# RMSNorm with SiLU on one core: the first store cut into four one-row transfers, two constants filled by GpSimd

## The chip, the core and the metric

The kernel runs on one core of a Trainium2 chip. The metric is the device time of one execution in microseconds (us). Before the change the median of three runs is 316.97 us (316.86 to 317.07).

A core has TensorE (matmuls), VectorE (DVE in the profile), ScalarE (ACT), GpSimd (POOL) and SyncE (SP, which here only issues DMAs). Sixteen DMA engines move data between the memory of the chip (HBM) and the core's working memory (SBUF, 128 partitions).

## The reference

The input x is 8 x 1024 x 2048 in float32, gamma has 2048 elements. Each of the 8192 rows is divided by its root mean square, multiplied by gamma, and put through SiLU:

```
rms = np.sqrt(np.mean(x ** 2, axis=-1, keepdims=True) + eps)
out = gamma * x / rms
return (out * (1 / (1 + np.exp(-out)))).astype(np.float32)
```

67.1 MB are read and 67.1 MB written.

## The kernel before, in words

The rows are cut into 16 blocks of 512. In a block each of the 128 partitions holds J = 4 rows that follow one another in HBM, so that a partition's part of a block is one run of 4 x 2048 float32 = 32 KB, and a block is 4 MB. Six buffers (BUFS) of that size lie in SBUF. `load(b)` (L54) is one DMA issued from ACT's queue into the next buffer; `store(b)` (L102) is one DMA issued from SP's queue out of it. The work is done in place in the buffer. Load b+6 goes into the buffer of block b, and so waits until store b has landed.

For each block there are these steps:

- `squares_scalar` (L65) and `squares_vector` (L73): the sums of squares of the four rows, one or two rows on ACT and the rest on VectorE.
- `root` (L82, ACT) and `invert` (L87, VectorE): square root of the mean plus eps, and its reciprocal.
- `multiply` (L92, VectorE): row times reciprocal times gamma, a row at a time.
- `silu` (L98, ACT): two instructions, each over two rows of a partition (128 x 4096); then the store.

The order is written out by hand (`manual_schedule`), and each engine works its own instructions in that order; an instruction that waits holds what is behind it in its engine's queue. ACT's queue holds the issues of the loads too: `squares_scalar(b + 1, loads)` issues load b+3 right behind the first of its rows, for b from 3 on. SP's queue holds gamma's DMA (L110) and then the 16 stores in order, each behind a wait for its block's last SiLU.

Ahead of the loop, load 0 is issued (L106). Then `ones` (128 x 128) and `eps_t` (128 x 1) are filled by VectorE (L107, L108). ACT squares one column of ones (L109), and TensorE multiplies ones by gamma (L113) to spread gamma over all partitions; VectorE copies the result (L115). Load 1 is issued behind L109, and loads 2 to 5 behind an ACT instruction that waits for that copy (L116). The last block is treated in a somewhat different order (L152 to L159) and ends with one store.

Of the kernel before, what the change touches and what calls it, by code (L numbers as in the profile page):

```python
# [1 line left out]

# [4 lines left out]

ACT = mybir.ActivationFunctionType
ALU = mybir.AluOpType


@with_exitstack
def kernel(
    ctx: ExitStack,
    tc: tile.TileContext,
    x: bass.AP,
    gamma: bass.AP,
    eps: bass.AP,
    out: bass.AP,
):  # L20

    nc = tc.nc
    P = nc.NUM_PARTITIONS
    f32 = mybir.dt.float32
    x2 = x.flatten_outer_dims()
    o2 = out.flatten_outer_dims()  # L30
    n, d = x2.shape
    J = 4
    BUFS = 6
    nblk = n // (P * J)
    xb = x2.rearrange("(b p j) d -> b p (j d)", p=P, j=J)
    ob = o2.rearrange("(b p j) d -> b p (j d)", p=P, j=J)

    singles = ctx.enter_context(tc.tile_pool(name="singles", bufs=1))
    pool = ctx.enter_context(tc.tile_pool(name="pool", bufs=BUFS))
    small = ctx.enter_context(tc.tile_pool(name="small", bufs=2))  # L40
    psum = ctx.enter_context(tc.tile_pool(name="psum", bufs=1, space=bass.MemoryType.PSUM))

    Q = 4
    w = d // Q
    g = singles.tile([P, d], f32)
    eps_t = singles.tile([P, 1], f32)
    ones = singles.tile([P, P], f32)
    junk_a = psum.tile([P, d], f32, name="junk_a")
    junk_v = psum.tile([P, d], f32, name="junk_v")
    blocks, sss, rmss, rstds = {}, {}, {}, {}  # L50

    def load(b):
        xt = pool.tile([P, J * d], f32, name="xt")
        nc.scalar.dma_start(out=xt, in_=xb[b])  # L54
        blocks[b] = xt

    def row(b, j):
        return blocks[b][:, j * d:(j + 1) * d]

    def squares_scalar(b, loads=()):  # L60


        sss[b] = small.tile([P, J], f32, name="ss")
        for j in range(share(b)):
            nc.scalar.activation(out=junk_a, in_=row(b, j), func=ACT.Square,  # L65
                                 accum_out=sss[b][:, j:j + 1])
            if j == 0:
                for s in loads:
                    load(s)

    def squares_vector(b):
        for j in range(share(b), J):
            nc.vector.tensor_tensor_reduce(  # L73
                out=junk_v, in0=row(b, j), in1=row(b, j), scale=1.0, scalar=0.0,
                op0=ALU.mult, op1=ALU.add, accum_out=sss[b][:, j:j + 1])

    def share(b):
        return 1 if 4 <= b <= 12 and b % 2 == 0 else 2

    def root(b):  # L80
        rms = small.tile([P, J], f32, name="rms")
        nc.scalar.activation(out=rms, in_=sss.pop(b), func=ACT.Sqrt, scale=1.0 / d, bias=eps_t)  # L82
        rmss[b] = rms

    def invert(b):
        rstd = small.tile([P, J], f32, name="rstd")
        nc.vector.reciprocal(out=rstd, in_=rmss.pop(b))  # L87
        rstds[b] = rstd

    def multiply(b):  # L90
        for j in range(J):
            nc.vector.scalar_tensor_tensor(out=row(b, j), in0=row(b, j), scalar=rstds[b][:, j:j + 1],  # L92
                                           in1=g, op0=ALU.mult, op1=ALU.mult)

    def silu(b):
        for h in range(0, J, 2):
            cols = slice(h * d, (h + 2) * d)
            nc.scalar.activation(out=blocks[b][:, cols], in_=blocks[b][:, cols], func=ACT.Silu)  # L98
        store(b)

    def store(b):
        nc.sync.dma_start(out=ob[b], in_=blocks[b])  # L102

    with tc.manual_schedule():

        load(0)  # L106
        nc.vector.memset(ones, 1.0)  # L107
        nc.vector.memset(eps_t, float(eps))  # L108
        nc.scalar.activation(out=junk_a[:, 0:1], in_=ones[:, 0:1], func=ACT.Square)  # L109
        nc.sync.dma_start(out=g[0:1, :], in_=bass.AP(tensor=gamma.tensor, offset=gamma.offset, ap=[[d, 1], [1, d]]))  # L110
        for c in range(Q):
            cols = slice(c * w, (c + 1) * w)
            nc.tensor.matmul(junk_v[:, cols], ones[0:1, :], g[0:1, cols], start=True, stop=True)  # L113
        load(1)
        nc.vector.tensor_copy(out=g, in_=junk_v)  # L115
        nc.scalar.copy(out=junk_a[:, 0:1], in_=junk_v[:, d - 1:d])  # L116
        for b in range(2, BUFS):
            load(b)

        last = nblk - 1
        SOON = 3
        squares_scalar(0)
        squares_vector(0)
        root(0)
        invert(0)
        for b in range(last):
            loads = [b + 3] if BUFS <= b + 3 < nblk else []
            if b < SOON:  # L130
                multiply(b)
                squares_scalar(b + 1, loads)
                silu(b)
                squares_vector(b + 1)
                root(b + 1)
            elif b < last - 1:
                squares_scalar(b + 1, loads)
                squares_vector(b + 1)
                root(b + 1)
                multiply(b)  # L140
                silu(b)
            else:
                multiply(b)
                squares_scalar(b + 1)
                silu(b)
                squares_vector(b + 1)
                root(b + 1)
            if b + 1 < last:
                invert(b + 1)


        for j in range(J):  # L152
            if j == J // 2:
                invert(last)
            nc.vector.tensor_mul(out=row(last, j), in0=row(last, j), in1=g)  # L155
        for j in range(J):
            nc.scalar.activation(out=row(last, j), in_=row(last, j), func=ACT.Silu,  # L157
                                 scale=rstds[last][:, j:j + 1])
        store(last)  # L159


# [1 line left out]
_INS = ['x', 'gamma', 'eps']  # L163
_OUTS = [((8, 1024, 2048), 'float32')]

_NUMBERS = {'eps': 9.999999747378752e-06}


# [26 lines left out]
```

## Time and profile before

| What | Before |
|---|---|
| Median of three runs | 316.97 us (316.86 to 317.07) |
| Span of the profiled execution, first to last instruction | 315.1 us |
| What lies between the two | 1.9 us |
| HBM read, written | 67.12 MB, 67.11 MB |
| Mean over the span | 426 GB/s |
| First store issued, last store issued | 35.2 us, 300.9 us |
| Load 6 (the first into a used buffer) issued | 66.7 us |

The profile gives a time of its own for the span alone; the runs' time includes what lies ahead of the first instruction and behind the last one.

The page has a row for each engine's busy time, a picture of the span in 40 slices (one digit each, busy tenths; 9 is 90% or more), the DMA queues with packets, MB and the share of the 16 engines' time, and the chain of work that ended last. The view of windows gives, for a stretch, its length, the busy time of each engine (in brackets the number of its instructions), TensorE's granted clock, the busy share of the DMA engines (over 1 where packets that start in the stretch end behind it) and GB/s. A line of the timeline has start, duration, engine (ACTq and SPq are the queues that issue DMAs), line of the code, operation, out<-in, count. The trace also holds every DMA packet with queue, size, start and duration; a packet here is one partition's run.

### The profile page before, as it was taken

What the parts mean: (1) busy time and instruction counts of PE and PEld (TensorE: products, weight loads), DVE (VectorE), ACT (ScalarE), POOL (GpSimd) and SP (SyncE); (2) the same over time, 40 slices, a digit from 0 to 9 for tenths busy, and PEclk for the clock granted to TensorE, in tenths of its full rate; (3) what the DMA queues carried; (4) which work ended last, traced back from release to release, by engine and by line L of the source; (5) the groups of instructions that cost most, each with busy time, mean ns of one, the idle gap of its engine ahead of it and who ended that gap; (6) DMA issues with size and microseconds to landing.
All of it is one profiled execution on the core that took longest, in us unless ns stands there. A gap on an engine that the chain in (4) does not pass through costs nothing.

```text
span 315.1 us, 439 instructions
## 1 busy us (share of the span) xinstructions
PE 7.2 (2%) x8; PEld 2.5 (1%) x8; DVE 235.3 (75%) x157; ACT 213.9 (68%) x137; POOL 0.2 (0%) x4
## 2 busy tenths in 40 slices
PE   6200000000000000000000000000000000000000
PEld 2000000000000000000000000000000000000000
DVE  0679697979895695957969489593995939999600
ACT  1269998972799258682687827877278768779910
POOL 0000000000000000000000000000000000000000
DMA  8999999999999999999999999999999999999997
GB/s 334 412 453 416 383 458 408 462 403 462 403 459 408 454 412 458 408 462 403 462 403 462 408 458 408 458 408 458 416 449 416 449 416 449 428 437 428 437 428 308
DMA packets 4613, 134.24 MB, mean 426 GB/s; under 512 B 514, under 2 KB 514, under 8 KB 514
## 3 DMA queue, kind: packets, MB, share of 16 engines
q10 hardware_dynamic: 2304, 67.11, 49.8%
q1 hardware_dynamic: 2306, 67.12, 49.3%
q14 instruction: 3, 0.02, 0.0%
HBM read 67.12 MB, written 67.11 MB: 426 GB/s over the span
## 4 chain that ended last, share of the span: by engine, by line
DMA 68%; DVE 14%; ACT 11%; issue 1%; ACTq 1%; DVEq 0%
DMA xt<-in_x_dram 68%; DVE xt L92 9%; DVE junk_v L73 5%; ACT xt L98 4%; ACT junk_a L65 3%; ACT xt L157 2%; ACT L82 1%; ACTq L190 1%; ACT L157 0%; ACT L98 0%; ACT rms L82 0%; DVE ss L73 0%; ACTq L54 0%; DVE rstd L87 0%; ACT L109 0%
## 5 line engine op out<-in xcount | busy, mean ns | idle before, releaser
L92 DVE SCALAR_TENSOR_TENSOR xt<-xt,rstd,g 128x2048 f32<-128x2048 f32 x60 | 137.0, 2346 | 0.1
L98 ACT ACTIVATE xt<-xt 128x4096 f32<-128x4096 f32 x30 | 108.3, 3615 | 27.4 <-DVE xt L92 27.4
L73 DVE CUSTOM_DVE_ANT_0 junk_v<-xt 128x2048 f32<-128x2048 f32 x37 | 85.1, 2299 | 42.9 <-DMA xt<-in_x_dram 42.2
L65 ACT ACTIVATE junk_a<-xt 128x2048 f32<-128x2048 f32 x27 | 50.7, 1876 | 16.1 <-DMA xt<-in_x_dram 14.0
L82 ACT ACT_TABLE_LOAD x15 | 19.2, 1283 | 26.6 <-DVE ss L73 26.5
L98 ACT ACT_TABLE_LOAD x14 | 18.0, 1283 | 0.2
L115 DVE COPY g<-junk_v 128x2048 f32<-128x2048 f32 x1 | 2.3, 2292 | 9.0 <-PE junk_v L113 9.0
L87 DVE RECIPROCAL rstd<-rms 128x4 f32<-128x4 f32 x16 | 2.7, 172 | 8.4 <-ACT rms L82 8.4
L155 DVE TENSOR_TENSOR xt<-xt,g 128x2048 f32<-128x2048 f32 x4 | 8.9, 2277 | 0.0
L82 ACT ACTIVATE rms<-ss,eps_t 128x4 f32<-128x4 f32 x16 | 4.8, 297 | 5.7 <-DVE ss L73 5.5
L157 ACT ACTIVATE xt<-xt,rstd 128x2048 f32<-128x2048 f32 x4 | 7.7, 1991 | 0.0
L113 PE MATMUL junk_v<-g,ones 1*128 1x512 f32 x8 | 7.2, 1072 | 2.8 <-DMA g<-in_gamma_dram 2.8
L116 ACT COPY junk_a<-junk_v 128x1 f32<-128x1 f32 x1 | 0.1, 144 | 9.8 <-DVE g L115 9.8
L73 DVE DVE_READ_ACCUMULATOR2_ANT ss<- 128x1 f32 x37 | 5.2, 141 | 0.0
L65 ACT ACTIVATION_READ_ACCUMULATOR junk_a<-xt 128x1 f32 x27 | 5.0, 186 | 0.0
L113 PEld LDWEIGHTS junk_v<-g,ones 1*128 1x128 f32 x8 | 2.5, 325 | 5.9 <-issue 5.9
L109 ACT ACT_TABLE_LOAD x1 | 1.3, 1283 | 1.1 <-PEq L176 1.1
L157 ACT ACT_TABLE_LOAD x1 | 1.3, 1283 | 0.0
L107 DVE MEMSET ones<- 128x128 f32 x1 | 0.2, 165 | 0.8 <-PEq L176 0.8
L109 ACT ACTIVATE junk_a<-ones 128x1 f32<-128x1 f32 x1 | 0.2, 174 | 0.0
L176 POOL MEMSET const-bfloat16-1.0<- 128x1 bf16 x1 | 0.1, 103 | 0.0
L176 POOL MEMSET const-uint8-127<- 128x1 uint8 x1 | 0.1, 102 | 0.0
(3 smaller groups left out, 0.3 us busy)
## 6 DMA issues: line engine op xcount, KB each, us to landing
xt<-in_x_dram ACTq DMA_DIRECT2D x16, 4096.0 KB, 38.7
out_dram<-xt SPq DMA_DIRECT2D x16, 4096.0 KB, 29.0
g<-in_gamma_dram SPq DMA_DIRECT2D x1, 8.0 KB
```

Of the source, the lines that this page charges most:

```text
L65: nc.scalar.activation(out=junk_a, in_=row(b, j), func=ACT.Square, accum_out=sss[b][:, j:j + 1])
L73: nc.vector.tensor_tensor_reduce(out=junk_v, in0=row(b, j), in1=row(b, j), scale=1.0, scalar=0.0, op0=ALU.mult, op1=ALU.add, accum_out=sss ...
L82: nc.scalar.activation(out=rms, in_=sss.pop(b), func=ACT.Sqrt, scale=1.0 / d, bias=eps_t)
L87: nc.vector.reciprocal(out=rstd, in_=rmss.pop(b))
L92: nc.vector.scalar_tensor_tensor(out=row(b, j), in0=row(b, j), scalar=rstds[b][:, j:j + 1], in1=g, op0=ALU.mult, op1=ALU.mult)
L98: nc.scalar.activation(out=blocks[b][:, cols], in_=blocks[b][:, cols], func=ACT.Silu)
L109: nc.scalar.activation(out=junk_a[:, 0:1], in_=ones[:, 0:1], func=ACT.Square)
L113: nc.tensor.matmul(junk_v[:, cols], ones[0:1, :], g[0:1, cols], start=True, stop=True)
L115: nc.vector.tensor_copy(out=g, in_=junk_v)
L155: nc.vector.tensor_mul(out=row(last, j), in0=row(last, j), in1=g)
L157: nc.scalar.activation(out=row(last, j), in_=row(last, j), func=ACT.Silu, scale=rstds[last][:, j:j + 1])
L190: with _tile.TileContext(nc) as tc:
```

## The change

Store 0 is no longer one DMA of 32 KB runs. Behind each half of block 0's SiLU, SP issues two DMAs of one row each (128 partitions x 8 KB). All other stores stay as they were. The two constants are filled by GpSimd instead of VectorE.

```
@@ silu(b)
         for h in range(0, J, 2):
             cols = slice(h * d, (h + 2) * d)
             nc.scalar.activation(out=blocks[b][:, cols], in_=blocks[b][:, cols], func=ACT.Silu)
-        store(b)
+            if b == 0:
+                for j in (h, h + 1):
+                    nc.sync.dma_start(out=ob[b][:, j * d:(j + 1) * d], in_=row(b, j))
+        if b:
+            store(b)
@@ start
         load(0)
-        nc.vector.memset(ones, 1.0)
-        nc.vector.memset(eps_t, float(eps))
+        nc.gpsimd.memset(ones, 1.0)
+        nc.gpsimd.memset(eps_t, float(eps))
```

## The prediction

> **What bounds the kernel now.** I read the page from the top, then the windows, the timeline and the records of single DMA packets. The page first:
>
> ```profile
> span 315.1 us, 439 instructions
> PE 7.2 (2%) x8; PEld 2.5 (1%) x8; DVE 235.3 (75%) x157; ACT 213.9 (68%) x137; POOL 0.2 (0%) x4
> ...
> DMA  8999999999999999999999999999999999999997
> ...
> q10 hardware_dynamic: 2304, 67.11, 49.8%
> q1 hardware_dynamic: 2306, 67.12, 49.3%
> ```
>
> No compute engine is full, but the DMA row holds a 9 in all but the first and last slice, and the two queues (q10 the loads issued by ACT, q1 the stores issued by SP) together occupy the 16 engines for 99.1% of the span. The chain of waits says the same: 68% of it is the loads of xt. Next, the windows by stage; the last two numbers of a row are DMA share and GB/s:
>
> ```profile
> 29.20:35.20 6.00, 0.00 (x0) 0.00 (x0) 4.75 (x5) 5.98 (x3) 0.00 (x0) 1.00 1.01 437
> 35.20:39.50 4.30, 0.00 (x0) 0.00 (x0) 2.67 (x3) 4.26 (x5) 0.00 (x0) 1.00 0.96 328
> ...
> 60.00:280.00 220.00, 0.00 (x0) 0.00 (x0) 176.30 (x118) 150.46 (x93) 0.00 (x0) 1.00 1.00 434
> ```
>
> Loads alone run at 437 GB/s and loads with stores at 434: the engines move the same bytes a second whatever the mix. Only the 4.3 us in which the first store joins are poorer, by 4.3 x (1 - 328/434) = 1.05 us.
>
> The packet records give the same as a sum. A DMA here is 128 packets of 32 KB, 8 on each engine, and a packet follows the last one after 1.210 us. 256 packets are 309.8 us. The first starts 1.8 us into the span and it and its neighbours are stretched by 1.2; the first store costs every engine 0.9 to 1.0; two 8 KB instruction fetches add 0.3 on one engine; from the last packet to the end are 1.2. Sum 315.2, against a span of 315.1. The median of the three runs, 316.97, is 1.9 longer than the span; I take those 1.9 as fixed, and forecast changes on the median.
>
> So only three things can move the time: bytes per second, the 0.9 at the first store, and a stretch in which both queues are empty. Compute counts only through the last.
>
> **The change, part by part.** The places are these rows of the timeline:
>
> ```profile
> 28.03 7.12 ACT L98 ACTIVATE xt<-xt 128x4096 f32<-128x4096 f32 x2
> ...
> 35.18 0.37 SPq L102 DMA_DIRECT2D out_dram<-xt  x1
> ...
> 66.72 0.34 ACTq L54 DMA_DIRECT2D xt<-in_x_dram  x1
> ```
>
> *The constants.* VectorE's memset of ones takes 0.165 us and ends at 0.99, that of eps_t 0.06. GpSimd's four one-column memsets take 0.10 each; none of 128x128 is shown, so the cost is between 0.1 and a value I can't read. It hardly matters: ones is first used by ACT at 2.43 (after a table load) and by TensorE at 2.75 (gamma lands at 2.5), so 1.7 us after 0.8 are covered. Were GpSimd slower, load 1 and loads 2 to 5 would be issued later than 1.21 and 12.38, but their packets' turns come at 12.0 and 21.7; nine more microseconds are covered. Cost 0; VectorE saves 0.2 us where it waits until 10 anyway.
>
> *The issue.* Three more DMA issues on SP, 0.33 us each: two at 31.65 (end of the first half of Silu), two at 35.18. SP's next work, store 1, comes at 49.83. Cost 0. The waits behind them are the Silu halves, which SP awaited before as well.
>
> *Three more completions per engine.* The 4-byte packet that ends a DMA takes 9 ns: 0.03 us.
>
> *Smaller packets.* Store 0 becomes 32 packets of 8 KB per engine instead of 8 of 32 KB. The nearest rows are the 8 KB instruction fetches within the run, recorded with 0.309 us, while a 32 KB packet is recorded with 1.213. A period is 3 ns shorter than its record, so 32 x 0.306 - 8 x 1.210 = 0.11 us. The other end comes from what these fetches took from their engine: the neighbouring packets were stretched so that the fetches cost 0.36 and 0.42 us, 0.05 and 0.12 more than 8 KB at 27.1 bytes/ns (0.303); 32 times that is 1.7 to 3.9 us. I take 0.11, as those two were a third queue's packets, fetched one at a time.
>
> The Trainium skill ("DMA: Bandwidth & Descriptors", section Anatomy of one DMA) speaks against cutting transfers: about 2.0 us fixed per DMA plus bytes at 436 GB/s. By that, were the costs in series, three more DMAs would be an estimated +6 us. This trace disagrees for queued ones: from store 13's last packet to store 14's first (293.38 to 293.75 on the earliest engines) nothing is lost.
>
> *The turn-taking.* With both queues full the records alternate, one load packet, one store packet. With 8 KB on one side a round is 1.210 + 0.306 = 1.516 us, of which the loads get four fifths. The first store packet, 4.4 us after its issue before, comes at about 36.1 instead of 39.6. 27 of the first six loads' 48 packets per engine have then started; the other 21 take 21 x 1.516 and end at 68 (83.7 before). By then 21 of 32 store packets are out, the other 11 go alone until 71.3, and with 1.5 us to land (as before) store 0 is done at 72.8 instead of 58.6. That is later than 66.72, when ACT issues load 6 into the same buffer. So ACT's queue stands 6 us at L54, with root(4) behind it; but root(4) needs VectorE's squares, which end at 75.4. 2.6 us of cover are left. Load 7, issued at 85.3, will wait for store 1 (ends near 86, lands 87.6): 2.3 us late, and beside it VectorE squares rows until 90. From there each load waits for its store; loads and stores both move every 19.4 us, and the next load is queued some 8 us before the last one ends.
>
> What is late next? The load queue is empty from 68 to about 76. The store queue isn't: the rest of store 0, store 1 (issued at 49.8) and store 2 (65.5) lie in it, so the engines stay full. The loads then run ahead: load 15 ends near 270 instead of 277.6, so the last store, issued at 300.9 for a turn at 303.4, gets some 7 us more cover. The end is still bytes over rate.
>
> Sum: 0 + 0 + 0.03 + 0.11 = +0.14, **317.1 us**. The 0.9 of the first store I leave as it is, only 3.5 us earlier.
>
> **The rivals.**
>
> *A. Rejoining costs (slower).* The load queue runs empty and comes back at about 76 among running stores, the mirror of the first store among running loads. If each join stops the engines, load 6 brings 0.55 (mean stretch of load 0's first packets) to 1.0: +0.7 to +1.1, 317.7 to 318.1. For it: both starts in this trace were dear. Against it: both were first uses, and no row shows a rejoin. It decides from the point where load 5 ends before store 0 has landed, 68 against 72.8 here. If the engines took turns otherwise, say so that a row's 8 packets pass together, the queue wouldn't run dry and A falls.
>
> *B. Dear small packets (slower).* 0.05 or more lost per 8 KB: +1.7 to +3.9, 318.7 to 320.9.
>
> *C. A cheaper first store (faster).* If the 0.9 is the filling of a pipe by the store's first packet, a packet of a quarter fills it with less: down to -0.7 with the 0.14 paid, 316.3. Against it: the 32 KB of store 1 may ask for the rest later.
>
> *D. The half store holds ACT.* If the second half of Silu had to wait until rows 0 and 1 have been read out (16 rounds of 1.516 from 36.1 on, landing near 62), ACT would stop for 30 us and both queues would run empty: store 1, 14.7 us after store 0, is then issued near 80 and store 2 near 96, while the 5 us of rows 2 and 3 and the loads are out by 72: 8 + 5 us idle, about 330. Against it: on block 1 Silu's first half starts at 42.00 while VectorE still multiplies rows 2 and 3 (to 46.15), so waits go by rows of a tile, not by the tile.
>
> *E. The fixed cost per DMA,* here three more joints in the store queue. If a joint stopped the engines until the last transfer had landed (1.5 us after its last packet), that were 4.6 with the 0.14, 321.6. Against it: 15 such joints in this trace show no gap, and the loads' packets would fill one. This is the page's rule as a mechanism of this kernel.
>
> **How the numbers follow.** Forecast 0.50 (317.1, within 0.2%); A 0.23; B 0.10; C 0.13; D 0.02; E 0.02. 0.2% is 0.63 us, about what a measurement of this kernel can tell from no change. A lies beyond it (317.60) with 0.18 of its 0.23, B, D and E wholly (0.14); C is beyond 316.34 with about half (0.07). Slower 0.32, faster 0.07, same the rest, 0.61. The range runs from C's end to B's lower end, 316.2 to 318.7; outside are the dear part of B, D and E.
>
> **What would show it.** In the profile after: the DMA row still 9 throughout, q1 with 2,738 packets instead of 2,306 (384 more of data, 48 more of completion); the first store issues at 31.65 and 35.18; load 6 issued at 72 to 73 rather than 66.72 and root(4) not later than 75.6; GB/s near 434 from 40 on, with a poorer window near 76 if A holds and between 36 and 71 if B does; the window of the first store at 32 to 36 as poor as before unless C holds. A SP or ACT wait of tens of microseconds at 32 would be D. The forecast is wrong if any slice in the middle loses its 9, or if 8 KB packets have a period over 0.32 us.

## The result, and the profile after

The changed kernel takes 318.02 us (median of six runs, 317.81 to 319.34); the kernel before, beside it, 317.02 (316.83 to 317.23). The ratio is 1.0042, with a 95% interval of 1.0029 to 1.0055: slower by 1.0 us, clear of the 0.2% that the prediction called no change. The profiled execution took 318.19, of which its span is 316.4; the span is 1.3 longer than before.

The page of the changed kernel, the lines that answer to those shown of before:

```profile
span 316.4 us, 447 instructions
...
DMA  8999999999999999999999999999999999999995
...
q10 hardware_dynamic: 2304, 67.11, 49.5%
q1 hardware_dynamic: 2738, 67.12, 49.2%
```

The DMA row still has its 9s in every slice but the ends, and q1 has the 2,738 packets that were forecast. So the 1.3 us are no gap that a slice would show.

The timeline of the changed kernel around the change (rows of its queues, of GpSimd and of root(4)):

```profile
0.73 0.20 POOL L111 MEMSET ones<- 128x128 f32 x1 [0.29 <-POOLq L180]
...
31.66 4.33 SPq L101 DMA_DIRECT2D out_dram<-xt  x4
...
71.63 0.34 ACTq L54 DMA_DIRECT2D xt<-in_x_dram  x1
...
75.56 0.30 ACT L82 ACTIVATE rms<-ss,eps_t 128x4 f32<-128x4 f32 x1 [5.50 <-DVE ss L73]
```

GpSimd fills ones in 0.20 us and is done long before ACT's first use. The first store is issued at 31.66, load 6 at 71.63 instead of 66.72, and root(4) runs at 75.56, as before: the wait of ACT's queue was covered. The view of waits shows the new order of things:

```profile
ACT junk_a L65 <- DMA out_dram<-xt: 30.3, 4, 7.8
...
ACT L82 <- DMA out_dram<-xt: 20.4, 4, 5.7
```

50.7 us in which ACT stands behind a load that waits for a store (columns: total, times, longest). Before there was no such row. It looks like the cause, and the experiments show that it isn't.

**Where the time is.** The records of single packets of the one profiled execution tell it. Each of the 16 DMA engines works its packets one after another, so the records fall into 16 chains. A record doesn't name its engine; a chain is put together by letting each packet follow the one that ended just before it. What a chain lost is the sum of what its packets were longer than usual (1.213 us for 32 KB, 0.309 for 8 KB); these sums are good to about 0.02 us. Times count from the first instruction of each kernel's own profiled execution. Before and after:

```
                        first store   72 to 110 us   mean end of 16 chains   last end
before                      0.88          0.04              313.43            313.95
changed                     0.39          0.23              313.32            314.98
(us; the first two columns are means over the 16 engines)
```

The mean engine ends 0.1 us earlier than before. The first store costs it half a microsecond less, and a second stall, near 87 us, and the small packets give most of that back. But one engine ends 1.0 us after the slowest of before: it lost 0.20 at 75 us on a store's packet, 0.55 at 87, and 0.31, 0.32 and 0.35 at 107, 127 and 146, these four times on the second load packet behind the last packet of a store, while 15 engines ended at 313.7 or earlier. The records of that engine around 87 us:

```
start us   us      packet
83.42      1.213   load 6
84.62      1.213   store 1, its last on this engine
85.83      1.213   load 6
87.05      1.766   load 6
88.81      1.220   store 2, its first on this engine
```

The time is set by the slowest of 16 engines, not by bytes over rate.

### The profile page after: what moved, and what is told of

The parts are those of the page before. It is cut to its first block, busy times and chain, and to the rows that moved or that the text cites. A ratio compares the mean times of both kernels' runs of the same rounds, so it can differ in the third digit from the quotient of the medians.

```text
span 316.4 us, 447 instructions
## 1 busy us (share of the span) xinstructions
PE 7.2 (2%) x8; PEld 2.5 (1%) x8; DVE 235.3 (74%) x155; ACT 212.4 (67%) x137; POOL 0.4 (0%) x6
## 3 DMA queue, kind: packets, MB, share of 16 engines
q1 hardware_dynamic: 2738, 67.12, 49.2%
## 4 chain that ended last, share of the span: by engine, by line
DMA 57%; ACT 18%; DVE 13%; issue 3%; ACTq 1%
DMA out_dram<-xt 42%; DMA xt<-in_x_dram 15%; ACT xt L98 9%; DVE xt L92 8%; DVE junk_v L73 5%; ACT junk_a L65 3%; ACT L82 2%; ACT xt L161 2%; ACT L98 1%; ACTq L194 1%; ACT rms L82 1%; ACT L161 0%; ACTq L54 0%; DVE ss L73 0%; DVE rstd L87 0%
```

## The experiments

The comparisons are with runs of the kernel before on the same chip. "Stall after" is the mean loss per engine between 72 and 110 us, as in the table above; it and the last end come from one profiled execution of each kernel. The expectations name theories of the loss: the gate (loads that are issued only when a store has landed), the packets (8 KB runs cost by themselves), the join (a queue that starts beside a running one stops the engines) and the constants.

**e1: the constants alone.**

```
-        nc.vector.memset(ones, 1.0)
-        nc.vector.memset(eps_t, float(eps))
+        nc.gpsimd.memset(ones, 1.0)
+        nc.gpsimd.memset(eps_t, float(eps))
```

> Only the two constants go to GpSimd; store 0 stays one transfer. All theories but one: no change, 317.0 (316.8 to 317.2), since GpSimd's fills take 0.20 and 0.10 us and end before ACT's first use at 2.43. Should the constants carry the loss (theory of the constants), this run has all of it: 318.0.

317.04 against 316.94, ratio 1.0005 (0.9996 to 1.0013). The constants cost nothing.

**e2: the split alone.** The diff of the change without those four lines.

> Only store 0 is split; VectorE fills the constants. Theories of the gate (loads from load 7 on are issued when a store lands, and the slowest DMA engine loses 0.3 to 0.5 us at each of some of these issues) and of the packets (8 KB runs cost by themselves): both the whole loss, 318.0 (317.7 to 318.6). Theory of the constants: 317.0.

317.82 (317.35 to 319.03), ratio 1.0029 (1.0016 to 1.0042). The split carries the loss. In its profiled run the stall after is 0.82 us and falls on all engines; the last ends at 314.95.

**e3: two transfers of 16 KB runs.**

```
             nc.scalar.activation(out=blocks[b][:, cols], ..., func=ACT.Silu)
-        store(b)
+            if b == 0:
+                nc.sync.dma_start(out=ob[b][:, cols], in_=blocks[b][:, cols])
+        if b: store(b)
```

> Store 0 goes out as two transfers of two rows (16 KB runs), one behind each half of its Silu. A round of turns is 1.210 + 0.605 us, so store 0 needs 16 rounds, 29 us from about 36: it lands near 66.7, at the moment at which load 6 is issued anyway, and load 5 still has packets in its queue. Theory of the gate: load 6 is issued at 66.7 to 67, the load queue doesn't run dry, later loads are issued when a load lands as before, and no engine loses over 0.2 us behind 60: 317.0 or a little less (316.6 to 317.2). Theory of the packets: half as many extra packets, half of the loss, 317.5. Theory of the join (every first packet of a stream stops all engines): 317.0, as the loads don't rejoin.

317.02, ratio 1.0002 (0.9993 to 1.0010). Load 6 was issued when it was before, and its packets began 1.0 us after load 5's last:

```profile
66.72 0.33 ACTq L54 DMA_DIRECT2D xt<-in_x_dram  x1
...
84.97 0.33 ACTq L54 DMA_DIRECT2D xt<-in_x_dram  x1
```

No stall after (0.06). This fits the theory of the gate and that of the join. It speaks against a cost in proportion to the number of extra packets, which would have been half of the loss.

**e4: the same split on store 11.** `if b == 11` instead of `if b == 0`.

> Store 11 instead of store 0 goes out as four one-row transfers (8 KB runs). No load waits for stores 10 to 15. Theory of the gate: small packets cost only their 0.14 us, 317.1 (316.9 to 317.3). Theory of the packets: the loss is as large as with store 0, 318.0.

317.20, ratio 1.0009 (1.0001 to 1.0018): 0.26 us, some more than the 0.14 worked out, and far from 1.0. Small packets by themselves, 32 more per engine beside loads, are not the loss. After four runs the theory of the gate stood.

**e5: the gate without small packets.** One transfer of 32 KB runs, held back on SP by a small transfer that waits for the first half of block 1's Silu (`hold` is a spare tile of one column; the other stores stay as they were):

```
+            if b == 1 and h == 0:
+                nc.sync.dma_start(out=hold, in_=blocks[1][:, 0:1])
+                store(0)
```

> No small rows: store 0 is one transfer of 32 KB runs, but it stands on SP behind a transfer of one column of block 1 (4 bytes a partition, into a spare tile) that waits for the first half of block 1's Silu; so it is issued at 45.8 instead of 35.2. Turns one to one, first packet near 50, end near 70, landing near 71.5, as late as in the changed kernel; load 5 ends then too, so the load queue runs dry for some 6 us and from load 7 on loads are issued when a store lands. Theory of the gate: the loss is there without one small packet, 317.5 to 318.6. Theory of the packets: 317.0 (316.8 to 317.2).

316.95, ratio 1.0003 (0.9995 to 1.0012). **The theory of the gate falls here.** The rows of its queues and of its waits:

```profile
45.68 0.51 SPq L101 DMA_DIRECT2D hold<-xt  x1
...
46.24 42.29 SPq L107 DMA_DIRECT2D out_dram<-xt  x4
...
72.00 0.33 ACTq L55 DMA_DIRECT2D xt<-in_x_dram  x1
...
87.69 0.34 ACTq L55 DMA_DIRECT2D xt<-in_x_dram  x1
```

```profile
ACT junk_a L66 <- DMA out_dram<-xt: 29.5, 4, 7.4
...
ACT L83 <- DMA out_dram<-xt: 20.3, 4, 5.4
```

Load 6 comes at 72.00 and load 7 at 87.69 (71.63 and 87.42 in the changed kernel), ACT's waits for stores add up to 49.8 us (50.7), and no load packet moved between 63.2 and 76.0, a longer gap than the changed kernel's 67.7 to 75.7. Yet the stall after is 0.04. In this kernel neither the gate nor the dry queue nor the rejoin of load 6 costs anything by itself.

The kernel differs from its plan in one thing. Store 0 was issued at 46.24, but its first packet starts at 60.24 and not near 50. From 49.58 on the store queue holds the 128 packets of 4 bytes of `hold`, 8 on each engine, and each took a turn against a whole load packet of 32 KB. So store 0 ran beside loads for 3 us only, and alone until 71.6.

**e6: the gate with five buffers.** `BUFS = 5`.

> Five buffers instead of six, all stores whole. From load 5 on each load waits for the store of five blocks before, whose landing comes after the load's place in ACT's order; the load queue should not run dry. Theory of the gate in its wide form (loads issued at a store's landing cost, dry queue or not): 317.5 or more, with lost time behind 60 us on single engines. In its narrow form (the queue must first run dry): 317.0. Theory of the packets: 317.0.

316.94, ratio 1.0001 (0.9992 to 1.0010), stall after 0.04, with even more waiting of ACT:

```profile
ACT junk_a L65 <- DMA out_dram<-xt: 39.9, 6, 7.4
...
ACT L82 <- DMA out_dram<-xt: 22.0, 4, 5.6
```

The load queue didn't run dry here, so this supports e5 in one half: loads that wait for stores cost nothing. The sixth buffer buys nothing in this kernel.

**e7: four rows behind both halves.** The four issues were moved behind the second Silu in the program.

```
+        if b == 0:
+            for j in range(J):
+                nc.sync.dma_start(out=ob[b][:, j * d:(j + 1) * d], in_=row(b, j))
+        else:
+            store(b)
```

> Four one-row transfers, but all behind the second half of Silu, so that store 0 starts when it did before. 18 loads' packets per engine are left, 18 rounds of 1.516, so the loads end near 67, store 0 near 71.3 and lands near 72: the gate holds as in the changed kernel. Theory of the gate: 318.0 (317.5 to 318.6). Theory of the packets: 318.0. If the early start is what costs: 317.0.

318.02, ratio 1.0037 (1.0025 to 1.0050). It did not do what it was meant to:

```profile
31.65 4.38 SPq L101 DMA_DIRECT2D out_dram<-xt  x4
```

Rows 0 and 1 need only the first half's data, and SP has nothing ahead of them, so they go at 31.65 all the same. It is a repetition of e2 (stall after 0.57, last end 314.70); whether an early start matters, it doesn't tell.

**e8: one row of 8 KB, then 24 KB runs.**

```
+            nc.sync.dma_start(out=ob[b][:, :d], in_=row(b, 0))
+            nc.sync.dma_start(out=ob[b][:, d:], in_=blocks[b][:, d:])
```

> Store 0 as one row (8 KB runs) and then the other three (24 KB runs), both behind the second half of Silu. 8 rounds of 1.516 and 8 of 2.118 from 39.6: the store ends near 68.5 if the loads last so long; load 5 ends near 71.5, as 18 packets are left. Store 0 lands near 70, load 6 is issued then, before load 5 has ended, so the load queue doesn't run dry, though the load waits for the store. Theory of the gate, narrow form (dry queue): 317.0 or up to 0.3 less, if the first store's join is cheaper with small packets (it cost 0.3 to 0.5 per engine in the changed kernel, 0.9 to 1.0 before). Wide form: 317.2 to 318.

317.10, ratio 1.0007 (0.9998 to 1.0016), stall after 0.05. The first row went at 31.60 again, so load 6 could go at its old time:

```profile
31.60 0.36 SPq L100 DMA_DIRECT2D out_dram<-xt  x1
...
35.11 0.33 SPq L101 DMA_DIRECT2D out_dram<-xt  x1
...
66.70 0.34 ACTq L54 DMA_DIRECT2D xt<-in_x_dram  x1
```

Its join was paid in two parts: 0.25 with the 8 KB packets, 0.39 between 45 and 56, where the 24 KB packets begin. That suggested a new theory, the filling: small rows pay only a part of the first store's join, and the rest falls due later. Its rival: small packets that outlast the load queue cost, whatever went before. The next three kernels were built for these two.

**e9: store 1 in rows, store 0 whole.** `if b == 1`.

> Store 0 goes out whole, store 1 as four one-row transfers. The first store then joins as before (about 0.9 us on every DMA engine near 36 to 39); then store 1's small rows run beside loads 5 and 6 from 59 on, four fifths of the engines' time go to the loads, the load queue ends near 88, store 1 near 92, and load 7 waits for it: small packets, a dry queue and waiting loads, as with store 0. Theory of the filling (the first store's join is paid by large packets; small rows pay a part of it, and the rest falls due later, unevenly over the engines, when the queue had run dry in between): the join was paid by store 0, so 317.1 (316.9 to 317.3), with no second stall. Theory of small and dry (small rows that outlast the load queue cost, whatever went before): 317.7 to 318.5, with a stall some 15 us behind the end of store 1.

317.93 (317.43 to 318.32), ratio 1.0030 (1.0019 to 1.0041). The first store paid its full join (0.87) and the loss came none the less: stall after 0.69, nearly all of it between 104 and 107, last end 314.90. No load packet had moved between 86.8 and 95.5. **The theory of the filling falls.**

**e10: 8 KB, 8 KB, 16 KB runs.**

```
+                for a, z in (((0, 1), (1, 2)) if h == 0 else ((2, 4),)):
+                    nc.sync.dma_start(out=ob[b][:, a * d:z * d], in_=blocks[b][:, a * d:z * d])
```

> Store 0 as two one-row transfers (8 KB runs) behind the first half of Silu and one of two rows (16 KB runs) behind the second. 16 rounds of 1.516 and then 1.815 from 36: the loads end near 69.5, the store near 71, so the load queue runs dry for some microseconds, less than with four rows. Theory of the filling: the join's rest is paid evenly near 60, where 16 KB packets begin to alternate with loads; little is left near 86: 316.9 to 317.3. Theory of small and dry: 317.4 to 318.2.

317.85 (317.60 to 318.00), ratio 1.0029 (1.0018 to 1.0040); stall after 0.53.

**e11: 16 KB, 8 KB, 8 KB runs.** The same with `((0, 2),)` and `((2, 3), (3, 4))`.

> Store 0 as one transfer of two rows (16 KB runs) behind the first half of Silu and two of one row (8 KB runs) behind the second. 16 packets of 16 KB pair with loads in turn (1.815 a round; 8 per engine), then 16 of 8 KB: the loads end near 70, the store near 71, the load queue runs dry as with four rows. Theory of the filling: the join is paid as with two halves (0.64 us per engine there, against 0.9 with a whole store and 0.2 to 0.4 with rows), so no more than 0.3 falls due later: 316.9 to 317.3. Theory of small and dry: 317.5 to 318.5.

317.95 (317.20 to 319.60), ratio 1.0036 (1.0019 to 1.0053); stall after 0.88. In both the load queue was dry (69.3 to 75.7 and 70.5 to 76.0 us), and load 6 came late, e10 first:

```profile
71.56 0.34 ACTq L54 DMA_DIRECT2D xt<-in_x_dram  x1
```

```profile
71.84 0.33 ACTq L54 DMA_DIRECT2D xt<-in_x_dram  x1
```

**e12: four transfers, 32 KB runs, late.** As e5, but store 0 in four groups of 32 partitions:

```
-                store(0)
+                for p in range(0, P, P // 4):
+                    nc.sync.dma_start(out=ob[0][p:p + P // 4], in_=blocks[0][p:p + P // 4])
```

> As the run with the delayed whole store 0 (32 KB runs, issued near 45.8, dry load queue near 70 to 76, load 6 near 72), but store 0 goes out as four transfers of 32 partitions each, with runs of 32 KB. The slow kernels so far have in common a store of several transfers and small packets, and a load queue that runs dry. Theory of small and dry: no small packet, so 317.0 (316.8 to 317.2), no stall near 86. Theory of many and dry (the number of transfers, not the size of the runs): 317.6 to 318.5, with the stall near 86.

325.55, ratio 1.0272 (1.0258 to 1.0286). **It doesn't tell the two apart**, since it brought a cost of its own. The windows (last number: GB/s):

```profile
46.00:60.00 14.00, 0.00 (x0) 0.00 (x0) 12.23 (x10) 12.60 (x9) 0.00 (x0) 1.00 1.01 407
60.00:80.00 20.00, 0.00 (x0) 0.00 (x0) 18.20 (x15) 8.48 (x6) 0.00 (x0) 1.00 1.01 292
110.00:280.00 170.00, 0.00 (x0) 0.00 (x0) 135.27 (x90) 116.17 (x73) 0.00 (x0) 1.00 1.00 433
```

While the quarters run, the engines move 292 GB/s with a busy share of 1.01: 20 x (1 - 292/433) = 6.5 us lost there alone. It has a stall behind that as well: between 89 and 95 us, 5 to 10 us after the loads came back at 84.1, load 6's packets are longer than usual by 1.0 us on the mean engine, most of it where store 1 ends and store 2 begins. That is the place of the stall in the slow kernels, and no data packet of this store is shorter than 32 KB. It speaks for the number of transfers, but with the disturbance just ahead it is no proof.

The other runs side by side, from the packet records; "dry" is whether the load queue had run empty, by over 3 us, before a load that waited for store 0 (for store 1 in e9; in e4 no load waits for store 11):

```
                     8 KB packets  dry   stall after  last end   ratio
before                    no       no       0.04       313.95      -
e1  constants             no       no       0.05       314.00    1.0005
e3  two of 16 KB          no       no       0.06       313.96    1.0002
e6  five buffers          no       no       0.04       314.27    1.0001
e5  whole, late           no       yes      0.04       314.00    1.0003
e4  store 11 in rows      yes      no       0.04       313.87    1.0009
e8  8 KB, then 24 KB      yes      no       0.05       314.00    1.0007
changed                   yes      yes      0.23       314.98    1.0042
e2  split alone           yes      yes      0.82       314.95    1.0029
e7  split again           yes      yes      0.57       314.70    1.0037
e9  store 1 in rows       yes      yes      0.69       314.90    1.0030
e10 8, 8, 16 KB           yes      yes      0.53       314.51    1.0029
e11 16, 8, 8 KB           yes      yes      0.88       314.99    1.0036
```

**What is shown:** in this table the loss goes with both, one-row transfers and a dry load queue behind them. It is in all six kernels that have both, and in none of the seven others. The changed kernel, e2 and e7 send the same transfers, so the six are four patterns; rows without a dry queue rest on e4 and e8, and a dry queue without rows on e5 alone. Between 60 and 94% of each stall lies at joints of two whole stores, above all where the first whole store that follows ends and the next begins, some 10 us after the loads have come back: there an engine works two load packets in a row, and one or both are stretched. The first store's stall in the kernel before lies in a like place, on the load packets just ahead of that store's first one. In e10 and e11 another 0.19 and 0.18 us fall between 72 and 80, where load 6 comes back. All of it is uneven over the engines.

**What stays open:** why. All six send the store in three or four transfers as well as in small runs. The one run meant to part these was disturbed by its narrow transfers, and it has a stall of the same kind without small runs, so the number of transfers stays a rival of their size. Nor is it shown why the stall waits for the end of the next whole store.

## Why the prediction was right or wrong, point by point

The time lies in the range (316.2 to 318.7), but not where the forecast put it: 317.1 and no change were forecast, 318.02 and slower came. That the range holds it is luck as far as the mechanism goes: the range was wide enough because of rivals A and B, and neither is what happened.

- *The constants, the issues, the cover of ACT:* right. e1 shows no cost; root(4) runs at 75.56 (75.58 before).
- *Smaller packets:* right in the row. Inside store 0 the 8 KB packets are recorded with 0.309 us. The 0.14 for all extra packets was 0.26 on store 11, in an interval (0.03 to 0.57) that holds it. Rival B is out.
- *The turn-taking:* right nearly to the number. A round took 1.517 us (load 4's first packet to load 5's, 43.79 to 55.92, over 8), the loads ended at 67.7 (forecast 68), store 0 at 71.1 (71.3), load 6 was issued at 71.63 (72.8), load 7 at 87.42 (87.6), and load 15 ended at 269.0 (270). The Trainium skill ("DMA: Bandwidth & Descriptors", section Queues, rings and completion order) says that each engine goes round between its queues packet by packet; the trace agrees, with 8 KB on one side and 32 on the other.
- *"So the engines stay full ... The end is still bytes over rate":* this is the step that failed. The engines stayed busy, but the sum had no term for a second stall, and it took the end of the mean engine for the end. In the changed kernel the mean engine did end on time (313.32 against 313.43); the slowest was 1.0 us late, and that is most of the 1.3 us by which the span grew. In the other five the mean is later too, by 0.1 (e7) to 0.8 (e9), and the last end by 0.6 to 1.0.
- *Rival A, the rejoin:* its time (317.7 to 318.1) came true, its mechanism in the main didn't. Between 72 and 80, where load 6 rejoined, the mean engine lost 0.02 us in the changed kernel, and e5 rejoins after a longer gap at no cost; only e10 and e11 lose something there (0.19 and 0.18). Its point of decision, a load queue that ends before the store has landed, is one half of the condition that the runs show; the other half, the store in several transfers of short runs, it lacked.
- *Rival C, a cheaper first store:* half true. The join does get cheaper with smaller packets: 0.71 (e4) to 0.88 us per engine with 32 KB, 0.65 to 0.71 with 16 KB (e3, e11), 0.25 to 0.45 with 8 KB (changed, e2, e7). No median shows a gain from it; e3, which had only this, stands at 1.0002. The slowest engine, again, ends no earlier (313.96 in e3, 313.95 before). By its own picture, a quarter of the filling, the gain would have been 0.5 to 0.6 us with the 0.14 paid, not 0.7.
- *Rival D* didn't occur: rows 0 and 1 went out at 31.66 and ACT's second half of Silu followed at once.
- *Rival E* isn't it either: e4 has the same three more joints. Before, none of the 15 joints cost more than 0.02 us on any engine; the first engine passes the one quoted in the prediction at 293.75. The section of the Trainium skill quoted there gives its figure for DMAs issued from GpSimd, and these are issued from SP. But the loss that came does lie mostly at a joint, that of the next two whole stores.

## What to carry to other kernels

Where the DMA engines are full from end to end, as here, starting a transfer earlier gained nothing, and the picture of busy slices didn't tell the two kernels apart: look at when each of the DMA engines ends, since the slowest sets the time. Cutting a transfer into short runs does not only change its own length; it hands its turns to the other queue, and what that other queue then does (here it ran ahead and dry) has to be followed through the buffers. And a cause that fits the place and the time, as the waits for stores did here, is worth the run that makes it without the change: e5 had the same waits to within a microsecond, and no loss.

## What the runs showed of the hardware that was not expected

- Stores that read 32 partitions at a time run far slower than stores over all 128: 292 GB/s against 433 in the windows of e12, with the engines no less busy. The Trainium skill ("SBUF — State Buffer", section Door 1: The DMA port swizzle) states that partitions 0 to 31 reach only 8 of the 16 ports, for an asymptote of about 218 GB/s; between 64 and 77 us, where the quarters run almost alone, the window view gives 224 GB/s, near that figure, so the trace agrees.
- The first store's stall grows with its packets, as given under rival C, and moves with it: in e5, where the first store's packets begin at 60.24, the 0.8 us lie between 56 and 60, on load packets.
- Tiny packets take whole turns: in e5 the 8 packets of 4 bytes and the completion on each engine held the store behind them for over 10 us (49.58 to 60.24), while the loads ran ahead.
- A transfer issued on SP waits for its data and for what is ahead of it on SP, not for the place of its line among ACT's instructions: rows 0 and 1 in e7 and row 0 in e8 left SP at 31.6, with the issue written behind the second Silu.
- Some of the kernels with the loss scatter more than the kernel before: 317.2 to 319.6 in e11, 317.8 to 319.3 in the changed kernel, against 316.8 to 317.2 before, beside the latter. Others don't: 317.6 to 318.0 in e10. Whether the same engine is caught each time isn't shown, as each kernel has one trace and the records don't name engines.
